# A mixer's attention steps spread over earlier products, and its branches taken attention by attention

## The chip, the cores and the metric

One core of a Trainium2 chip runs the whole program as a single launch. The metric is device time in microseconds (us). Of the kernel before, three runs were timed: 2173.23, 2173.37 and 2174.28, median 2173.37. One more execution was profiled; it took 2171.94.

## The reference, cut to what matters

The program is a stack of ten blocks on 256 tokens of width 1024: six of a first network (feed-forward, token mixer, feed-forward, twice) and four of a second one. The change touches only the token mixer, which runs twice (stages 1 and 4). A mixer has three attentions ("branches") on the same input, a gate for each, and one output projection:

```
proj = hn @ w_in                                   # q,k,v twice, c_q, c_kv, k_rope, gates
y_a = from_heads(moba_attention(partial_rope(qa), partial_rope(ka), va))      # 256 keys: a causal softmax
y_b = from_heads(stick_breaking_attention(qb, kb, vb))
qc = to_heads(rms_norm(c_q, q_norm) @ w_uq); kv = to_heads(rms_norm(c_kv, kv_norm) @ w_ukv)
y_c = from_heads(causal_softmax_attention(qc, [k_nope, kr], vc))
g = sigmoid(gates + b_gate)
merged = einsum('bsnk,nkd,bsnd->bsd', [y_a, y_b, y_c], w_branch, g)
return merged @ w_out
# stick breaking, per head, z = q k / 8, strictly earlier keys only:
log_1m = where(mask, log_sigmoid(-z), 0); suffix = reversed cumsum(log_1m) - log_1m
w = where(mask, exp(log_sigmoid(z) + suffix), 0);  y = w @ v
```

## The kernel before, in words

**Products.** Every weight arrives as 512 KB units of 128 x 1024 float32 (queue SP, line 81). ScalarE (ACT) rounds a unit to fp32r (`hi`, L122), VectorE (DVE) subtracts for the rest (`lo`, L127), and TensorE (PE) makes each product in three matmuls (L332 to L334). `lin2` does both halves of the 256 tokens against a block of four units: 8 chunks of the contraction, 6 matmuls each, so 12 matmuls a unit and 48 a block. `lin` does one half. Matmuls L332 to L334 are called "products" below; those of the latent projections are 384 or 416 columns wide, the others 512. Modulation vectors are made on DVE beside this (L422). Units are split ahead of their use as far as buffers allow.

**Queued steps.** What is not such a product is cut into steps (closures) in the queue `side`. `tick` runs the next step; `lin2` calls it once a unit, that is once in 12 products, unless its argument `fine` is set: then once in 6, and twice in 6 while the queue holds more than `backlog` steps. The order of instructions on every engine is fixed by the order in which this Python code issues them; engines run their own lists in order and wait on semaphores.

**A mixer** goes: q, k, v of attention 0 (three blocks), which queues its steps; q, k, v of attention 1, which queues the stick-breaking steps; the latent block (`lin2` with 416 columns), whose normed rows `cs` are transposed to `cT` (L374); gate block 0; the projections of the latent attention (`lin` with 384 and 512 columns in four rounds; queries `qs` and keys `ks` are transposed by L383 and copied by ACT); gate blocks 1 to 5; then twelve branch products (`branch(h, n, t)`: half `h` of the output columns, attention `n`, half `t` of the tokens); the transposes of the merged sum; and the output product.

**Softmax steps** (`softmax_steps`, attentions 0 and 2, three items each): score (PE L850, L853, maxima on DVE L876, eight or four exponentials on ACT L879), norm (DVE L887, L890), transposes of p (PE L383) with a copy (ACT L897), and the product with v (PE L913).

**Stick-breaking steps** (`stick_steps`, attention 1, two groups of four heads): three scores (PE L959, ACT L961, L962), one step for all three with Ln on ACT (L967), a sum on DVE (L968) and the mask product on GpSimd (POOL, L970); two empty steps (`yield`); then three steps with the triangular product (PE L976, L979, L980) and Exp (ACT L982); at the end two products with v (PE L991).

`branch` cannot start before its attention is ready; until then it runs queued steps back to back:

```
        def branch(h, n, t):
            while n not in ready:
                self.tick()
```

Of the kernel before, what the change touches and what calls it, by code (L numbers as in the profile page):

```python
# [15 lines left out]
AF = mybir.ActivationFunctionType  # L16
# [171 lines left out]
class Net:  # L188
# [759 lines left out]
    def stick_steps(self, groups, q_of, k_of, v_of, split):  # L948


        nc = self.nc
        w_of = {}
        for heads in groups:
            banks = [(1, heads, P, P), (0, heads[:2], 256, 0), (0, heads[2:], 256, 0)]
            zs, sps = [], []
            for kt, hs, w, q0 in banks:
                z = self.ps("acc")
                for i, h in enumerate(hs):
                    nc.tensor.matmul(z[:, i * w:(i + 1) * w], k_of(h, kt), q_of(h, q0, 256), start=i == 0, stop=False, skip_group_check=True)  # L959
                a = self.t2(name="sp")  # L960
                nc.scalar.activation(a, z, AF.Abs)  # L961
                nc.scalar.activation(a, a, AF.Exp, scale=-1.0)  # L962
                zs.append(z)
                sps.append(a)
                yield
            for (kt, hs, w, q0), z, a in zip(banks, zs, sps):
                nc.scalar.activation(a, a, AF.Ln, bias=1.0)  # L967
                nc.vector.scalar_tensor_tensor(out=a, in0=z, scalar=0.0, in1=a, op0=ALU.max, op1=ALU.add)  # L968
                d = a.rearrange("p (h q) -> p h q", q=w)[:, :, :P]
                nc.gpsimd.tensor_tensor(out=d, in0=d, in1=self.ustrict[:, None, :].broadcast_to([P, len(hs), P]), op=ALU.mult)  # L970
            yield
            yield
            for (kt, hs, w, q0), z, a in zip(banks, zs, sps):
                z3 = z.rearrange("p (h q) -> p h q", q=w)
                n = len(hs)
                nc.tensor.matmul(z, self.ntri, a, start=False, stop=False, skip_group_check=True)  # L976
                if kt == 0:
                    j = heads.index(hs[0])
                    nc.tensor.matmul(z3[:, :, P:], self.nones, sps[0].rearrange("p (h q) -> p h q", q=P)[:, j:j + n], start=False, stop=False, skip_group_check=True)  # L979
                nc.tensor.matmul(z3[:, :, :P], self.identb, self.m_causalT[:, None, :].broadcast_to([P, n, P]), start=False, stop=True, skip_group_check=True)  # L980
                e = self.t2(name="w")
                nc.scalar.activation(e, z, AF.Exp)  # L982
                for i, h in enumerate(hs):
                    w_of[h, kt] = e[:, i * w:(i + 1) * w]
                yield
        for m in range(2):
            yp = self.ps("acc")
            for c in range(2):
                for kt in range(NT):
                    for h in (4 * m + 2 * c, 4 * m + 2 * c + 1):  # L990
                        nc.tensor.matmul(yp[(h % 2) * 64:(h % 2) * 64 + 64, c * 256 + kt * P:(c + 1) * 256], v_of(h, kt), w_of[h, kt],  # L991
                                         start=kt == 0, stop=kt == 1, skip_group_check=True)
            self.soon(lambda m=m, yp=yp: split(m, yp), 1)
            yield

    def plan_mixer(self, st):
        l, A = st // 3, self.A
        blk = lambda b: [(A["w_mix"][l, b, u], U) for u in range(4)]
        w = []
        for b in range(6):  # L1000
            w += blk(b)
        w += [(A["w_mla"][l, u], 832) for u in range(4)] + blk(6)
        w += [(A["w_uq"][l, u], 768) for u in range(2)] + [(A["w_ukv"][l], U)]
        for b in range(7, 12):
            w += blk(b)
        for h in range(2):
            for n in range(3):
                w += [(A["w_branch"][l * 3 + n, h, u], U) for u in range(2)]
        return w + [(A["w_out"][l, k], U) for k in range(KC)]

    def mixer(self, st, pre, rest):
        nc = self.nc
        l = st // 3
        A = self.A
        self.reserve = 8
        hp = lambda h: slice((h % 2) * 64, (h % 2) * 64 + 64)
        par = lambda y: y.rearrange("p (c two d) -> p two c d", two=2, d=64)
        yTs, ready = {}, set()
# [16 lines left out]

        def put(n, i, ps, whole=False):

            if i == 0:
                yTs[n] = [self.s4([P, 4, 256], F32R, "yT") for _ in range(2)]
            if whole:  # L1040
                self.split_T(ps, *(a[:, 2 * i:2 * i + 2] for a in yTs[n]))
            else:
                self.split_T(ps, *yTs[n], i)
            if i:
                ready.add(n)

        def attend(n, q, k, v):

            if n == 0:
                self.both(self.softmax_steps(  # L1050
                    self.EVEN_ODD, lambda h, t: q[hp(h), h // 2, t * P:(t + 1) * P], lambda h, m: k[hp(h), h // 2, :m],
                    lambda: v, self.m_causal, lambda t, ps: put(n, t, ps)), lambda: self.free(q, k))
                self.side.append(lambda: self.free(v))
            else:
                gen = self.stick_steps(
                    [list(range(g, 8, 2)) for g in range(2)], lambda h, a, b: q[hp(h), h // 2, a:b],
                    lambda h, kt: k[hp(h), h // 2, kt * P:(kt + 1) * P], lambda h, kt: v[:, kt, h * 64:(h + 1) * 64], lambda m, ps: put(n, m, ps, True))
                self.steps(gen, 16)
                self.side.append(lambda: self.free(q, k))
                self.steps(gen, 2)  # L1060
                self.side.append(lambda: self.free(v))
# [5 lines left out]
        for n in range(2):  # L1067
            q, k = (self.s4([P, 4, 256], F32, "qkT") for _ in range(2))
            v = self.s4([P, NT, 512], F32, "v")
            if n == 0:  # L1070
                uq = self.get(4)
                end = rest(2)
                head(0, 0, self.lin(h8[0], uq), True, q)
                end()
                uk = self.get(4)
                head(1, 0, self.lin(h8[0], uk), True, k)
                self.trans(pre, 1)
                self.rate = 1
                head(0, 1, self.lin(h8[1], uq, drop=True), True, q)
                head(1, 1, self.lin(h8[1], uk, drop=True), True, k)  # L1080
            else:
                for i, dst in enumerate((q, k)):
                    for t, ps in enumerate(self.lin2(h8)):
                        head(i, t, ps, False, dst)
            for t, ps in enumerate(self.lin2(h8)):
                nc.scalar.copy(v[:, t], ps)
            attend(n, q, k, v)

# [3 lines left out]
        def gate(b):  # L1092
            h, n = divmod(b, 3)
            bg = self.t2(name="bg")
            nc.gpsimd.dma_start(bg, A["bgate"][l * 3 + n, h].partition_broadcast(P))
            g = self.s4([P, NT, 512], F32, "g")
            for t, ps in enumerate(self.lin2(h8)):
                nc.vector.tensor_tensor(out=g[:, t], in0=ps, in1=bg, op=ALU.add)
            gs[h, n] = g

# [4 lines left out]
        cs = [self.t2(name="cs") for _ in range(NT)]  # L1105
        css = self.sm(4, name="css")
        parts = [(0, 256), (256, 384)]
        for t, ps in enumerate(self.lin2(h8, 416)):
            nc.scalar.copy(cs[t][:, :416], ps[:, :416])
            junk = self.t2(name="junk")  # L1110
            for i, (a, b) in enumerate(parts):
                nc.scalar.activation(junk[:, a:b], cs[t][:, a:b], AF.Square, scale=(b - a) ** -0.5, accum_out=css[:, 2 * t + i:2 * t + i + 1])
# [22 lines left out]
        for hb in range(2):  # L1135
            for t in range(NT):
                c = lambda i: lambda k: [a[:, k + i, t * P:(t + 1) * P] for a in cT]
                ps = self.lin(c(0), wq, 384, 2, 1, hb * 384, 0)
                s = self.t2(name="qs")
                nc.scalar.activation(s[:, :384], ps[:, :384], AF.Copy, scale=96 ** -0.5)  # L1140
                sv = s[:, :384].rearrange("p (h d) -> p h d", h=4)[:, :, 64:96]
                self.rope(sv, sv, self.col("cosm", t * 32, 32), self.col("sinm", t * 32, 32), 4, 16)
                ps = self.lin(c(2), [wk], 512, 1, 1, hb * 512, 0)
                self.tick()
                pv = ps.rearrange("p (h d) -> p h d", h=4)
                z = self.t2(name="ks")
# [25 lines left out]
        def branch(h, n, t):  # L1172
            while n not in ready:
                self.tick()
            if (h, n) not in ub:
                ub[h, n] = self.get(2)
                nc.scalar.activation(gs[h, n], gs[h, n], AF.Tanh, scale=0.5)
            g = gs[h, n][:, t]
            ps = self.lin(lambda k: [a[:, k, t * P:(t + 1) * P] for a in yTs[n]], ub[h, n], 512, 4, 2)
            m = merged[t][:, h * 512:(h + 1) * 512]  # L1180
# [15 lines left out]
                self.split(pt.rearrange("p (k c) -> p k c", k=4), mT[0][q][s], mT[1][q][s], self.half)  # L1196
            self.free(merged[t])

        for n in range(3):
            for t in range(NT):  # L1200
                branch(0, n, t)
        for n in range(3):
            branch(1, n, 0)
        branch(1, 0, 1)
        mT = self.pair8("mT")
        mtrans(0)
        branch(1, 1, 1)
        branch(1, 2, 1)
        return self.proj_out(st, mT, lambda: mtrans(1))

# [965 lines left out]
```

## Time and profile before

| what | value |
|---|---|
| median of three runs | 2173.37 us |
| profiled execution, its own time | 2171.94 us |
| its span, first to last instruction | 2170.2 us |
| mean granted TensorE clock (1 is 2.4 GHz) | 0.975 |
| matmuls x9858, busy | 2050.8 us, 94% of the span |
| DVE busy | 1363.1 us, 63% |
| ACT busy | 917.4 us, 42% |
| DMA, mean rate | 274 GB/s |

The span is what the sums below move; 1.7 us lie around it. A busy share is a mean over stages. A timeline row gives the start, the duration, the engine, line, operation and tiles; in square brackets stands how long the engine had been idle before it and which instruction released it. Matmuls overlap, so a duration is a little longer than the distance to the next start.

### The profile page before, as it was taken

To read this page: it belongs to the slowest core of one execution; us is meant where nothing else is said; L and a number is where in the kernel's file an instruction comes from. 1 tells how busy PE (TensorE), PEld (TensorE's weight loads), DVE (VectorE), ACT (ScalarE), POOL (GpSimd) and SP (SyncE) were. 2 spreads that over 40 slices of the span, in tenths; PEclk is the share of its full clock that TensorE was granted. 3 is DMA by queue.
4 is the path that set the end of the run, shared out by engine and by line. 5 is a ranking of instruction groups with operands and counts; after the bars stand their busy time and mean duration, and the time that the engine had idled before them with its cause. 6 is when DMAs were issued, how large, how long until landed. Compare 5 with 4: busy or idle time off the path is not lost. (4 is left out here: it accounts for less than half of the span.)

```text
span 2170.2 us, 27088 instructions
## 1 busy us (share of the span) xinstructions
PE 2050.8 (94%) x9858; PEld 1437.9 (66%) x9858; DVE 1363.1 (63%) x2108; ACT 917.4 (42%) x1635; POOL 89.6 (4%) x118
## 2 busy tenths in 40 slices
PE   7999999988999999999989899998899989989998
PEld 4888777766888788777767688776533337763333
DVE  4976877558965886687647886697422258742223
ACT  3544454555544544355465544464211026621110
POOL 1000001000000000000000000030000002000000
PEclk9999999989999999999999999999899999989999
DMA  9987686527886787676635687666699996759998
GB/s 390 325 286 239 238 293 236 171 82 250 321 300 211 253 321 251 217 265 213 239 115 197 248 311 253 217 225 231 238 419 419 384 409 190 256 201 419 419 386 329
DMA packets 166956, 595.08 MB, mean 274 GB/s; under 512 B 18744, under 2 KB 18832, under 8 KB 166816
## 3 DMA queue, kind: packets, MB, share of 16 engines
q1 hardware_dynamic: 162864, 582.16, 72.8%
q0 software_dynamic: 2064, 6.88, 1.2%
q10 hardware_dynamic: 1888, 4.24, 0.6%
q8 instruction: 80, 1.31, 0.2%
q14 instruction: 60, 0.49, 0.1%
HBM read 590.00 MB, written 3.20 MB: 273 GB/s over the span
## 5 line engine op out<-in xcount | busy, mean ns | idle before, releaser
L127 DVE TENSOR_TENSOR lo<-raw,hi 128x1024 fp32r<-128x1024 f32 x478 | 570.3, 1214 | 37.0 <-ACT hi L122 35.5
L332 PE MATMUL psw<-hi,hT 128*128 128x512 f32 (+1 forms) x1296 | 525.8, 406 | 10.4 <-ACT hT L617 9.6
L334 PE MATMUL psw<-lo,hT 128*128 128x512 f32 (+1 forms) x1296 | 507.8, 392 | 5.9 <-DVE lo L127 5.8
L333 PE MATMUL psw<-hi,hT 128*128 128x512 f32 (+1 forms) x1296 | 507.6, 392 | 0.0
L122 ACT CAST hi<-raw 128x1024 fp32r<-128x1024 f32 x478 | 479.1, 1047 | 51.0 <-DMA raw<-in_w_gu_dram 16.9
L332 PEld LDWEIGHTS psw<-hi,hT 128*128 128x128 f32 x1296 | 244.7, 189 | 75.5 <-ACT hT L617 13.5
L334 PEld LDWEIGHTS psw<-lo,hT 128*128 128x128 f32 x1296 | 244.5, 189 | 59.6 <-DVE lo L127 8.5
L333 PEld LDWEIGHTS psw<-hi,hT 128*128 128x128 f32 x1296 | 245.2, 189 | 46.2
L422 DVE SCALAR_TENSOR_TENSOR aacc<-raw,csil,aacc 128x1024 f32<-128x1024 f32 x196 | 250.5, 1278 | 0.0
L1592 PE MATMUL psw<-raw,hg 128*64 128x512 f32 x1024 | 238.7, 605 | 5.7 <-PEq L2024 3.8
L1592 PEld LDWEIGHTS psw<-raw,hg 128*64 128x64 f32 x1024 | 69.0, 138 | 131.4 <-issue 122.5
L332 PE MATMUL psacc<-hi,gT 128*128 128x512 f32 x352 | 139.9, 397 | 6.0 <-ACT gT L725 3.1
L334 PE MATMUL psacc<-lo,gT 128*128 128x512 f32 x352 | 138.8, 394 | 1.0 <-DVE lo L127 1.0
L333 PE MATMUL psacc<-hi,gT 128*128 128x512 f32 x352 | 139.0, 395 | 0.0
L1636 DVE TENSOR_TENSOR x<-x,psacc 128x512 f32<-128x512 f32 x64 | 43.0, 686 | 121.3 <-PE psacc L1632 121.3
L1611 PE MATMUL psacc<-raw,gT 128*64 128x512 f32 x448 | 104.7, 598 | 0.4 <-DMA raw<-in_moe_d_dram 0.4
L688 ACT ACTIVATE sg<-psw 128x256 f32<-128x256 f32 x86 | 32.7, 384 | 153.9 <-PE psw L334 152.5
L557 POOL TENSOR_TENSOR r<-m,nhalf 128x1 f32<-128x1 f32 (+3 forms) x30 | 45.4, 1512 | 1218.1 <-DVE m L554 815.1
L689 DVE TENSOR_TENSOR sg<-psw,sg 128x256 f32<-128x256 f32 x86 | 35.9, 422 | 92.8 <-ACT sg L688 92.7
L725 ACT CAST gT<-psw 128x256 fp32r<-128x256 f32 x88 | 29.5, 375 | 130.0 <-PE psw L383 130.0
L332 PEld LDWEIGHTS psacc<-hi,gT 128*128 128x128 f32 x352 | 66.9, 190 | 22.1 <-ACT gT L725 4.8
L334 PEld LDWEIGHTS psacc<-lo,gT 128*128 128x128 f32 x352 | 66.9, 190 | 15.8 <-DVE lo L127 1.9
(331 smaller groups left out, 2314.1 us busy)
## 6 DMA issues: line engine op xcount, KB each, us to landing
raw<-in_ada_dram SPq DMA_DIRECT2D x224, 512.0 KB, 4.8
raw<-in_w_gu_dram SPq DMA_DIRECT2D x176, 512.0 KB, 4.9
raw<-in_moe_g_dram SPq DMA_DIRECT2D x128, 512.0 KB, 9.9
raw<-in_moe_u_dram SPq DMA_DIRECT2D x128, 512.0 KB, 9.9
raw<-in_moe_d_dram SPq DMA_DIRECT2D x128, 512.0 KB, 9.9
raw<-in_w_mix_dram SPq DMA_DIRECT2D x96, 512.0 KB, 4.6
raw<-in_w_dn_dram SPq DMA_DIRECT2D x88, 512.0 KB, 4.6
raw<-in_w_qkv_dram SPq DMA_DIRECT2D x48, 512.0 KB, 4.8
```

The lines of the kernel that those rows point to most:

```text
L122: nc.scalar.copy(hi[:, :cols], raw[:, :cols])
L127: nc.vector.tensor_tensor(out=lo[:, :cols], in0=raw[:, :cols], in1=hi.bitcast(F32)[:, :cols], op=ALU.subtract)
L332: mm(ps, a[0], w[0], start=first, stop=False)
L333: mm(ps, a[1], w[0], start=False, stop=False)
L334: mm(ps, a[0], w[1], start=False, stop=last)
L422: nc.vector.scalar_tensor_tensor(out=acc, in0=raw, scalar=c, in1=acc, op0=ALU.mult, op1=ALU.add)
L557: nc.gpsimd.tensor_tensor(out=r, in0=m, in1=self.nhalf[:, :w], op=ALU.pow)
L688: nc.scalar.activation(sg[:, :256], ps[:, :256], AF.Silu)
L689: nc.vector.tensor_tensor(out=sg[:, 256:], in0=ps[:, 256:], in1=sg[:, :256], op=ALU.mult)
L1592: mm(ps[s], hg(k, j)[:, s], w[0][:, i * 512:(i + 1) * 512], start=k == 0, stop=k == KC - 1)
L1611: mm(yb[h][s], gT[:, f * P + s.start:f * P + s.stop], w[0][:, h * 512:(h + 1) * 512], start=f == 0, stop=f == 3)
L1636: nc.vector.tensor_tensor(out=self.x[:, t, s], in0=self.x[:, t, s], in1=ps, op=ALU.add)
```

## The change

Six things, all in the mixer. The mixer's `lin2` calls get `fine=True`, with `backlog` 20, so a queued step runs after each 6 products, two while more than 20 wait. The first group of stick breaking has four empty steps in place of two between mask and triangular product. In the latent projections each `lin` runs a step at its middle and end. Branch products go attention by attention (both column halves of attention 0, then of 1, then of 2), with the weight units in that order, and both halves' gates go through tanh at once. The buffers of `yT` are taken by whichever part comes first.

```diff
-            yield
-            yield
+            for _ in range(4):
+                yield
...
-        for h in range(2):
-            for n in range(3):
+        for n in range(3):
+            for h in range(2):
                 w += [(A["w_branch"][l * 3 + n, h, u], U) for u in range(2)]
...
-        self.reserve = 8
+        self.reserve, self.backlog = 8, 20
...
-            if i == 0:
+            first = n not in yTs
+            if first:
                 yTs[n] = [self.s4([P, 4, 256], F32R, "yT") for _ in range(2)]
...
-            if i:
+            if not first:
                 ready.add(n)
...
-                self.steps(gen, 16)
+                self.steps(gen, 20)
...
-                    for t, ps in enumerate(self.lin2(h8)):
+                    for t, ps in enumerate(self.lin2(h8, fine=True)):
                         head(i, t, ps, False, dst)
...
-        for t, ps in enumerate(self.lin2(h8, 416)):
+        for t, ps in enumerate(self.lin2(h8, 416, fine=True)):
...
-                ps = self.lin(c(0), wq, 384, 2, 1, hb * 384, 0)
+                ps = self.lin(c(0), wq, 384, 2, 1, hb * 384, 1)
...
-                ps = self.lin(c(2), [wk], 512, 1, 1, hb * 512, 0)
+                ps = self.lin(c(2), [wk], 512, 1, 1, hb * 512, 1)
...
-                nc.scalar.activation(gs[h, n], gs[h, n], AF.Tanh, scale=0.5)
+                if h == 0:
+                    for i in range(2):
+                        nc.scalar.activation(gs[i, n], gs[i, n], AF.Tanh, scale=0.5)
...
-        for n in range(3):
-            for t in range(NT):
-                branch(0, n, t)
-        for n in range(3):
-            branch(1, n, 0)
-        branch(1, 0, 1)
+        for n in range(2):
+            for h in range(2):
+                for t in range(NT):
+                    branch(h, n, t)
+        branch(0, 2, 0)
+        branch(1, 2, 0)
         mT = self.pair8("mT")
+        branch(0, 2, 1)
         mtrans(0)
-        branch(1, 1, 1)
         branch(1, 2, 1)
```

Every engine has as many instructions as before. Three places show what moves; names carry the program's own tile numbers, and rows of the first mixer stand for both.

PE, second group of stick breaking, before: it stands behind the gate blocks, in the first branch products.

```order
L959 MATMUL psacc_3838<-qkT_2450,qkT_2451 128x128 x4
L959 MATMUL psacc_3846<-qkT_2450,qkT_2451 128x256 x2
L959 MATMUL psacc_3852<-qkT_2450,qkT_2451 128x256 x2
L976 MATMUL psacc_3838<-sp_3843,ntri 128x512
L980 LDWEIGHTS identb
L980 MATMUL psacc_3838<-m_causalT,identb 128x512
L976 MATMUL psacc_3846<-sp_3849,ntri 128x512
```

The same group in the changed kernel: its scores were issued 6 and 3 products apart, ahead of these rows, and this is the middle of the latent projections (`psw` from `cT`).

```order
L334 MATMUL psw_3259<-lo_3089,cT_2920 128x384
L383 MATMUL psw_3266<-ident,qs_3244 96x128 x4
L332 MATMUL psw_3279<-hi_3119,cT_2920 128x512
L333 MATMUL psw_3279<-hi_3119,cT_2921 128x512
L334 MATMUL psw_3279<-lo_3120,cT_2920 128x512
L383 MATMUL psw_3283<-ident,ks_3255 96x128 x4
L976 MATMUL psacc_3186<-sp_3191,ntri 128x512
L980 LDWEIGHTS identb
L980 MATMUL psacc_3186<-m_causalT,identb 128x512
```

Before, nothing stands between last score and first triangular product; now 15 products do, 12 of them ahead of the transposes of `qs_3244`.

ACT, latent projections, before: only copies and scalings of the projections.

```order
L1140 ACTIVATE qs_3115<-psw_3108 128x384
L442 COPY zs_3131<-psw_3126 128x256
L1148 COPY ks_3133<-psw_3122 128x4x64
L1140 ACTIVATE qs_3144<-psw_3137 128x384
L1148 COPY ks_3164<-psw_3151 128x4x64
```

ACT, the same place in the changed kernel, with the stick steps of the second group ahead of the first scaling (L1141 was L1140).

```order
L961 ACTIVATE sp_3229<-psacc_3226 128x512
L962 ACTIVATE sp_3229<-sp_3229 128x512
L967 ACT_TABLE_LOAD
L967 ACTIVATE sp_3191<-sp_3191 128x512
L967 ACTIVATE sp_3212<-sp_3212 128x512
L967 ACTIVATE sp_3229<-sp_3229 128x512
L1141 ACTIVATE qs_3244<-psw_3222 128x384
L1149 COPY ks_3255<-psw_3251 128x4x64
```

The scaling that the transposes of `qs_3244` need now follows the Ln passes of the third score.

ACT, first softmax item of attention 0, before: v's two copies are out of the way before its exponentials.

```order
L1086 COPY v_2098<-psw_2350 128x512
L1086 COPY v_2098<-psw_2351 128x512
L122 CAST hi_2464<-raw_2413 128x1024
L442 COPY zs_2481<-psw_2476 128x256
L122 CAST hi_2492<-raw_2440 128x1024
L879 ACT_TABLE_LOAD
L879 ACTIVATE p_2519,rs_2504<-psacc_2505,mx_2517 128x128 x4
```

ACT there in the changed kernel (L1087 was L1086): the score was issued 6 products before v's block ends.

```order
L1087 COPY v_2098<-psw_2350 128x512
L1087 COPY v_2098<-psw_2351 128x512
L879 ACT_TABLE_LOAD
L879 ACTIVATE p_2487,rs_2472<-psacc_2473,mx_2485 128x128 x4
L879 ACTIVATE p_2494,rs_2472<-psacc_2474,mx_2492 128x128 x4
```

The exponentials now wait for the end of v's block; on PE the transposes of this item follow its score after 18 products and one further score, where it was 48 products.

## Rows read from the trace of the kernel before

**Rows 1.** Windows of the second mixer: us, busy PE, PEld, DVE, ACT, POOL, clock, DMA, GB/s.

```profile
932.00:1096.00 164.00, 161.83 (x840) 129.33 (x839) 117.07 (x158) 86.16 (x150) 7.04 (x12) 1.00 0.70 241
1096.00:1166.00 70.00, 59.52 (x309) 44.45 (x308) 37.74 (x53) 41.98 (x80) 5.28 (x6) 0.90 0.26 91
```

**Rows 2.** PE's waits in a mixer, by releaser: us in total, times, longest.

```profile
PE psacc L976 <- POOL sp L970: 6.6, 2, 5.9
PE psw L332 <- DVE cT L374: 2.7, 1, 2.7
```

**Rows 3.** Timeline of PE, second mixer, from the second stick group to the branches.

```profile
1106.16 2.88 PE L959 MATMUL psacc<-qkT,qkT 64*128 64x128 f32 x16
1114.97 2.08 PE L976 MATMUL psacc<-sp,ntri 128*128 128x512 f32 x2 [5.92 <-POOL sp L970]
...
1121.33 2.82 PE L991 MATMUL psacc<-w,v 128*64 128x256 f32 x32
1124.08 0.50 PE L332 MATMUL psw<-hi,yT 128*128 128x512 f32 x1
...
1126.96 1.95 PE L850 MATMUL psacc<-qkm,qkm 96*128 96x128 f32 x16
...
1131.91 1.89 PE L850 MATMUL psacc<-qkm,qkm 96*128 96x256 f32 x8
...
1133.90 1.23 PE L383 MATMUL psw<-ident,p 128*128 128x128 f32 x8
...
1148.01 0.80 PE L332 MATMUL psw<-hi,yT 128*128 128x512 f32 x1
...
1150.31 0.41 PE L334 MATMUL psw<-lo,yT 128*128 128x512 f32 x1
```

**Rows 4.** Timeline of PE, second mixer: the same kinds of step at full pace.

```profile
982.76 1.13 PE L850 MATMUL psacc<-qkT,qkT 64*128 64x256 f32 x8
983.82 0.39 PE L853 MATMUL psacc<-m_causal,identb 128*128 128x256 bf16 x2
986.82 1.03 PE L383 MATMUL psw<-ident,p 128*128 128x128 f32 x8
...
1008.80 1.09 PE L913 MATMUL psacc<-pT,v 128*64 128x128 f32 x16
1009.82 0.50 PE L332 MATMUL psw<-hi,hT 128*128 128x512 f32 x1
...
1104.67 1.02 PE L976 MATMUL psacc<-sp,ntri 128*128 128x512 f32 x2
```

**Rows 5.** Timeline of ACT and POOL behind those scores, up to the masks.

```profile
1110.92 1.28 ACT L967 ACT_TABLE_LOAD   x1
1112.22 1.67 ACT L967 ACTIVATE sp<-sp 128x512 f32<-128x512 f32 x3
...
1113.65 2.63 POOL L970 TENSOR_TENSOR sp<-sp,ustrict 128x512 f32<-128x512 f32 x3 [13.01 <-DVE sp L968]
```

**Rows 6.** Groups of instructions in the second mixer: count, busy us, mean ns, idle before.

```profile
L879 ACT ACTIVATE p<-psacc,mx 128x128 f32<-128x128 f32 x16 | 5.6, 376 | 4.7 <-DVE mx L876 4.7
L968 DVE SCALAR_TENSOR_TENSOR sp<-psacc,sp 128x512 f32<-128x512 f32 x6 | 3.8, 684 | 12.8 <-ACT sp L967 12.8
L1086 ACT COPY v<-psw 128x512 f32<-128x512 f32 x4 | 2.3, 594 | 0.6 <-PE psw L334 0.5
```

**Rows 7.** Timeline of PE, first mixer: the product behind the wait for `cT`.

```profile
340.25 0.44 PE L332 MATMUL psw<-hi,cT 128*128 128x384 f32 x1 [2.72 <-DVE cT L374]
```

**Rows 8.** A window of the first mixer after that wait; columns as in rows 1.

```profile
341.00:345.00 4.00, 4.00 (x19) 2.35 (x18) 2.93 (x12) 1.14 (x3) 1.01 (x4) 0.57 0.30 120
```

**Rows 9.** Timelines of POOL and DVE: one small POOL operation at two places, and DVE beside it.

```profile
1008.21 2.01 POOL L557 TENSOR_TENSOR r<-m,nhalf 128x4 f32<-128x4 f32 x1 [69.86 <-DVE m L554]
...
1008.03 1.29 DVE L422 SCALAR_TENSOR_TENSOR aacc<-raw,csil,aacc 128x1024 f32<-128x1024 f32 x1
...
1513.57 1.01 POOL L557 TENSOR_TENSOR r<-m,nhalf 128x4 f32<-128x4 f32 x1 [25.38 <-DVE m L554]
```

More of the change, by code (lines that the diff above doesn't have):

```diff
@@ L1082, in mixer @@
                 for i, dst in enumerate((q, k)):
-                    for t, ps in enumerate(self.lin2(h8)):
+                    for t, ps in enumerate(self.lin2(h8, fine=True)):
                         head(i, t, ps, False, dst)
-            for t, ps in enumerate(self.lin2(h8)):
+            for t, ps in enumerate(self.lin2(h8, fine=True)):
                 nc.scalar.copy(v[:, t], ps)
@@ L1096, in gate @@
             g = self.s4([P, NT, 512], F32, "g")
-            for t, ps in enumerate(self.lin2(h8)):
+            for t, ps in enumerate(self.lin2(h8, fine=True)):
                 nc.vector.tensor_tensor(out=g[:, t], in0=ps, in1=bg, op=ALU.add)
```

## The prediction

> **What bounds the kernel.** I read the page's busy shares first: TensorE (PE) 94%, DVE 63%, ACT 42%. PE sets the time, so a microsecond is to be had only where PE waits or runs at a low clock. The windows of a mixer say where that is. In its front, 164 us of weight products, PE is busy 161.8 us at clock 1.00; in the 70 us behind it, where the queue is emptied and the branches run, PE is busy 59.5 us at clock 0.90 [rows 1]. PE's waits by releaser name two kinds in a mixer that the change touches: 6.6 us for the masks of stick breaking (two waits, one of them 5.9) and 2.7 us for `cT` [rows 2]. The timeline shows the rest: in the second mixer the last stick group starts at 1106.16 and its final products end as branch products begin at 1124.08; the latent softmax runs from 1126.96 to 1148.01; the five products behind it start 0.43 to 0.6 us apart, where twelve in a row at full pace take 2.88 (1124.08 to 1126.96), 0.24 each [rows 3]. Those stretches are what the change can win: each holds steps that wait for a chain through ACT, DVE and POOL with nothing else left for PE. The first mixer shows the same waits, so I count everything twice.
>
> **What the change gives.** It puts these steps among earlier products, where they should cost their pace alone. Per mixer:
> - Stick group 2: 17.92 us elapsed (1106.16 to 1124.08) [rows 3]. At pace: scores 2.88, three products with their masks at 1.49 each (1104.67 to 1106.16) [rows 3, 4], final products 2.82: 10.2 together. Gain 7.7; 5.92 of it is the wait, the rest half-pace work behind it.
> - Latent softmax: 21.05 elapsed, less 2.88 for twelve products inside it, 18.17. At pace: three scores at 1.99 each (1131.91 to 1133.90), three transposes at 1.03, three products with v at 1.09 [rows 3, 4]: 12.3. Gain 5.8.
> - The five slow products: 2.30 (1148.01 to 1150.31) against 1.20: gain 1.1.
> - Group 1's wait: 6.6 - 5.9 = 0.7, counted whole here; what stays of it stands below.
> - Each return to the product stream costs a longer first product, 0.50 where others have 0.41 [rows 3, 4]. Steps that stood back to back now return one by one, some 16 more breaks: 16 x 0.1 = 1.6 lost.
>
> Sum 7.7 + 5.8 + 1.1 + 0.7 - 1.6 = 13.7; two mixers 27.4.
>
> **What it costs.** A step costs only its pace if enough products stand between its halves. At twice the rate there are half as many between two steps. I go through the places by the issue order and compare the cover with the chain.
> - *First softmax item, attention 0.* The chain: six products to the end of v's block 1.4, two copies of v 2 x 0.59, a table load 1.28, eight exponentials at 0.376, two DVE passes at 0.68 [rows 5, 6]: 1.4 + 1.2 + 1.3 + 3.0 + 1.4 = 8.3. The cover in the first mixer: 18 products (4.3) and a further score, 1.13 + 0.39 [rows 4], 5.8. PE waits 2.5. A wait of such a size is not its own whole price: behind the 2.72 us for `cT` in the first mixer [rows 7] the granted clock stands at 0.57 for four microseconds [rows 8], near the 1.2 GHz level, which loses 4 x 0.43 = 1.7. So 2.5 + 1.7 = 4.2. In the second mixer 24 products (5.8 + 1.5 = 7.3) leave 1.0. Together 5.2.
> - *Stick group 1.* Four empty steps at one per 6 products equal two at one per 12: 24 products both times. The 0.7 stays, and the products are now those of 416 columns; I add 0.8. 1.5 x 2 = 3.0.
> - *The wait for `cT`.* It lies at the same block's end and its chain is the same; what stands between now differs by a step or two. Zero, between -4.4 (2.72 + 1.7 won) and +4.4.
> - *Stick group 2, in the latent projections.* Its bare chain (ACT, the table, three Ln, DVE's sum, POOL's masks) cost 5.92 of waiting where nothing covered it. In the first mixer only 12 narrow products stand ahead of transposes which need a scaling that ACT does behind the Ln passes: about 0.19 each by width, 2.3. It leaves 3.6, with the clock 1.7: 5.3. In the second mixer 18 narrow products and sums cover about 4.6: 1.3. Together 6.6.
> - *Latent softmax.* It now competes with DVE's splits and modulation sums. Such a sum takes 1.28 and may start ahead of a normalization: between 0 and 1.28 each time, taken 0.9 per mixer. 1.8.
> - *tanh of both halves at once* delays a copy on ACT by one half's length; the branch products hold several finished PSUM tiles ahead. Nothing; if a tile is missing, one tanh per attention.
> - *The weight units' order* changes which 512 KB unit comes when, not how many; in the tail DMA is 0.26 busy [rows 1]. Nothing.
>
> Sum 5.2 + 3.0 + 0 + 6.6 + 1.8 = 16.6.
>
> *Does DVE become the bound?* Its steps move from the tail to the front: two groups' sums, maxima, normalizations, copies, some 15 us per mixer (22 passes of 0.68). 117.1 us of 164 [rows 1] become 132 of about 185, 72% (the front is longer by the PE steps it takes in). Not on average.
>
> One pair of rows speaks against putting masks beside splits: a POOL operation, 128x4, shows 2.01 us where a DVE pass of 1.29 lies beside it and 1.01 where it has POOL and DVE to itself [rows 9]. So a POOL operation can lose about one DVE pass. The Trainium skill ("SBUF — State Buffer", section "SBUF: two separate sides") says that VectorE and GpSimd share a port pair under an exclusive lock, held for the whole instruction by whichever began first; the two durations agree with it. By the row, four groups have three masks each, so 12 x 1.28 = 15.4 us at worst. I leave it out of the sum: the first mask of a group stands behind a DVE sum that must end first anyhow, and the chains above are not late by one pass at every mask. It is a rival below.
>
> **Sum.** 27.4 - 16.6 = 10.8 us won: 2171.94 - 10.8 = 2161.1 for the profiled execution. The median of the runs is 1.4 above it, so **2162.5, say 2162**. What is uncertain in this case: the wait for `cT` (4.4 either way) and the clock's 1.7 at two waits, 3.4: its own range is 2154 to 2170.
>
> **Rivals** (all against the median).
> - *Everything is covered.* The chains were measured with queues full of other work; if they fit, the 16.6 vanish: 2173.4 - 27.4 = 2146, and with the `cT` wait gone as well 2141.6. For it: front PE is never without work, and splits stand two to five units ahead. Against: the cover of 2.3 us at stick group 2 is far under 5.92.
> - *DVE serves the queue late.* Engines go in order; a DVE sum that waits for ACT's table and Ln (1.28 + 1.67 [rows 5]) holds the splits behind it, and PE waits for a `lo`. Four groups, up to 2.95 each, 11.8; half of it, 5.9, gives 2168, all 2174. For: the splits' lead is short in places. Against: a unit of 12 products lasts 2.9, so a lead of two hides one such delay.
> - *Slower.* One mechanism: bare chains now stand in the front six times where they stood in the tail twice. The four stick groups and two first softmaxes each cost the bare 5.92 and the 1.7 of low clock, 7.6 x 6 = 45.6, plus 1.8 for the latent softmax, against 27.4: 20 us lost, 2193. It decides from (27.4 - 1.8) / 6 = 4.3 us for each of the six. Against: at five of the six 18 or more products stand between, 3.4 us or more of 5.9 to 8.3. I take its middle, 5.5 each (33 + 1.8 against 27.4): 2181.
> - *POOL and DVE slow each other.* The 15.4 us at the masks takes the 10.8 and a little more: 2173 if two thirds reach PE, 2178 if all do. Against: the masks cover part of each other's wait.
> - *It does not do what it says.* The queue may be emptied in the front, so that the same waits stand in front of the gates rather than after: no gain, 2171 to 2175. The order shows steps between products at both places, which speaks against it.
>
> **Chances.** Forecast case 0.48, all covered 0.16, DVE late 0.11, slower 0.12, POOL beside DVE 0.05, no effect 0.08. The measurement can tell about 0.2%, 4.3 us, so "same" is 2169.1 to 2177.7. Faster takes the forecast case but 0.03 of its upper edge, the covered case, and 0.09 of the late DVE: 0.45 + 0.16 + 0.09 = 0.70. Slower: the mechanism 0.12 and 0.01 of POOL beside DVE, 0.13. Same: the rest, 0.17. The range: low 2143, inside the covered case (0.06 of it left out), high 2175, which leaves out the slower cases' 0.13: 0.81 inside.
>
> **What would show it.** In the profile after, the tail's window (branches and output) should be near 1.00 of clock with no wait at L976, L383 or L913; the L976 wait for POOL should stand in the latent projections at 3 to 4 us in the first mixer, and a wait for p (L383 behind DVE L890) of 2 to 3 us near the first softmax. With everything covered, neither would be there. DVE late shows as PE waiting at L334 for `lo`; POOL beside DVE as masks well over the 0.88 us that each of three takes now (2.63 for three [rows 5]) and longer waits at L976. The slower case has six waits of over 4 us and a clock under 0.95 in the front. A mean front clock under 0.97, or a tail that still lasts 70 us, would make my account wrong whatever the time.

## The result, and the profile after

The changed kernel takes 2148.11 us (median of six, 2146.56 to 2154.43) against 2174.89 for the kernel before on the same chips (six, 2173.23 to 2177.83): ratio 0.9883, interval 0.9873 to 0.9894, about 25 us faster. The forecast was 2162, some 11 us faster, in a range of 2143 to 2175. The side and the range hold; the gain is more than twice what was forecast. The profiled execution took 2150.40, 21.5 less than that of before.

The page after, its busy times: the instructions and their cost are as before, the span is shorter.

```profile
span 2148.7 us, 27125 instructions
PE 2046.8 (95%) x9858; PEld 1436.9 (67%) x9858; DVE 1364.8 (64%) x2108; ACT 918.9 (43%) x1635; POOL 93.4 (4%) x118
```

The second mixer by windows, with the columns of [rows 1]: from 72 us behind its start, as there, to its branches, then the branches. These begin 28 us later in the mixer than before.

```profile
925.00:1116.00 191.00, 187.81 (x1019) 147.13 (x1018) 134.02 (x185) 118.40 (x219) 14.16 (x18) 1.00 0.63 211
1116.00:1150.00 34.00, 33.91 (x155) 27.94 (x154) 29.48 (x36) 17.80 (x19) 0.00 (x0) 1.00 0.60 218
```

The tail that PE spent at clock 0.90 with 10 us idle is now 34 us without a gap at 1.00; the stretch ahead of it is longer by the steps it took in, and DVE is busy 70% there (134.02 of 191), as estimated.

PE's waits in the mixers after, by releaser (us, times, longest), first mixer, then second; rows of the mixers' start, equal in both kernels, are left out.

```profile
PE psw L383 <- DVE qs L839: 4.9, 1, 4.9
PE psw L332 <- ACT zs L442: 2.0, 1, 2.0
...
PE psacc L976 <- POOL sp L970: 0.7, 1, 0.7
```

```profile
PE psw L440 <- ACT qs L1141: 1.4, 1, 1.4
...
PE psacc L976 <- POOL sp L970: 0.7, 1, 0.7
PE psw L383 <- DVE p L890: 0.6, 1, 0.6
...
PE psw L332 <- DVE g L1099: 0.5, 1, 0.5
```

Against [rows 2], the 5.9 at L976 and the wait for `cT` are gone in both mixers, and so are two kinds of wait in the tail that [rows 2] does not list, 2.4 at L913 and 1.5 at L383 for `p`; a new one of 4.9 stands at the transposes of `qs`, in the first mixer alone.

Where the time went is best read from PE's timeline, between the same rows in every kernel: *front*, from the last L483 ahead of the mixer to the first product on `cT`; *latent*, to the last on `cT`; *gates*, to the first on `yT`; *branches*, to the last on `yT`; *next*, from the last on `mT` to the next stage's L483. The output product between takes 22.6 or 22.7 everywhere. Each pair is first mixer / second.

| kernel | front | latent | gates | branches | next | sum with output |
|---|---|---|---|---|---|---|
| before | 111.7 / 159.9 | 10.9 / 9.0 | 67.2 / 67.0 | 74.6 / 75.9 | 68.0 / 69.8 | 355.1 / 404.2 |
| changed | 124.0 / 174.8 | 20.8 / 15.8 | 78.6 / 73.1 | 33.6 / 33.6 | 68.4 / 68.5 | 348.1 / 388.6 |
| old branches | 124.9 / 174.7 | 21.4 / 17.5 | 78.6 / 73.1 | 33.3 / 33.3 | 70.5 / 70.3 | 351.4 / 391.6 |
| coarse | 111.7 / 159.9 | 16.8 / 15.0 | 73.8 / 68.8 | 56.7 / 56.7 | 67.6 / 68.4 | 349.2 / 391.5 |
| two empty | 127.7 / 175.9 | 23.5 / 21.8 | 73.1 / 74.5 | 33.6 / 33.6 | 67.8 / 67.7 | 348.4 / 396.2 |
| quiet latent | 123.8 / 174.7 | 10.3 / 9.5 | 79.8 / 82.0 | 33.7 / 33.6 | 68.0 / 68.4 | 338.2 / 390.9 |
| late ticks | 123.7 / 174.7 | 19.8 / 16.2 | 78.5 / 73.1 | 33.6 / 33.7 | 68.5 / 67.3 | 346.8 / 387.6 |
| quiet, no double | 122.9 / 172.9 | 9.8 / 9.8 | 87.6 / 86.9 | 33.7 / 33.6 | 67.6 / 68.4 | 344.3 / 394.3 |
| order only | 111.4 / 160.0 | 10.8 / 9.0 | 67.2 / 66.9 | 73.0 / 72.9 | 68.4 / 68.4 | 353.5 / 399.9 |
| quiet first | 123.7 / 174.7 | 10.3 / 15.8 | 79.8 / 73.1 | 33.6 / 33.6 | 68.0 / 68.4 | 338.1 / 388.4 |

The two mixers with their next stages give 22.6 us (7.0 and 15.6); the branches alone lose 41.0 and 42.3, of which 33.6 and 27.9 come back as longer front, latent and gates. A second trace of the changed kernel, taken with the last experiments, has the same parts within 0.2, but for *next* in the second mixer (67.3).

### The profile page after: what moved, and what is told of

It is laid out like the page before. It is cut to its first block, busy times and chain, and to the rows that moved or that the text cites. A ratio compares the mean times of both kernels' runs of the same rounds, so it can differ in the third digit from the quotient of the medians.

```text
span 2148.7 us, 27125 instructions
## 1 busy us (share of the span) xinstructions
PE 2046.8 (95%) x9858; PEld 1436.9 (67%) x9858; DVE 1364.8 (64%) x2108; ACT 918.9 (43%) x1635; POOL 93.4 (4%) x118
## 5 line engine op out<-in xcount | busy, mean ns | idle before, releaser
L122 ACT CAST hi<-raw 128x1024 fp32r<-128x1024 f32 x478 | 480.8, 1048 | 91.6 <-PE psw L333 23.5
L1596 PEld LDWEIGHTS psw<-raw,hg 128*64 128x64 f32 x1024 | 68.6, 137 | 131.1 <-issue 122.9
L332 PEld LDWEIGHTS psacc<-hi,gT 128*128 128x128 f32 x352 | 67.4, 192 | 20.1 <-ACT gT L725 6.2
L333 PEld LDWEIGHTS psacc<-hi,gT 128*128 128x128 f32 x352 | 67.5, 192 | 16.1 <-DVE gT L727 2.4
```

Of the source, the lines that this page charges most:

```text
L122: nc.scalar.copy(hi[:, :cols], raw[:, :cols])
L332: mm(ps, a[0], w[0], start=first, stop=False)
L333: mm(ps, a[1], w[0], start=False, stop=False)
L1596: mm(ps[s], hg(k, j)[:, s], w[0][:, i * 512:(i + 1) * 512], start=k == 0, stop=k == KC - 1)
```

## Experiments

**Branches in the old order** (e1): branches, weight units and tanh as before, all else changed.

```diff
...
-        for n in range(2):
-            for h in range(2):
-                for t in range(NT):
-                    branch(h, n, t)
...
+        for n in range(3):
+            for t in range(NT):
+                branch(0, n, t)
+        for n in range(3):
+            branch(1, n, 0)
...
```

> The changed kernel with the old order of branches, of their weight units and of the tanh. Theory (the fine steps alone empty the queue before the gates end, so no branch waits for anything): 2148, between 2146 and 2151; no wait at L976, L913 or at L383 for p among the branch products. Rival (attention by attention is what gives the cover): 2158 or more, with waits of 2 us and more back between the gates and the output product.

Measured 2156.12, ratio 0.9912 (0.9899 to 0.9926): outside both. The theory's reason holds, since the branches have no wait and are even 0.3 shorter (33.3), but its number does not. Of the 6.3 that its mixers lose in the table, 3.9 stand in the *next* stage, 2.1 and 1.8. PE's waits there, from 515 to 535 us, of this kernel and then of the changed one:

```profile
PE psw L334 <- DVE lo L127: 3.0, 2, 2.2
PE psacc L332 <- ACT hi L122: 1.4, 1, 1.4
```

```profile
PE psw L383 <- DVE sg L689: 2.6, 1, 2.6
PE psacc L332 <- ACT gT L725: 0.5, 1, 0.5
```

With the old order the next stage's products wait for `lo` and `hi`. These waits go with the order and not with the length of the tail, for the kernel before has them too (518 to 538 us):

```profile
PE psw L334 <- DVE lo L127: 3.5, 2, 2.1
PE psacc L332 <- ACT hi L122: 1.5, 1, 1.5
```

There the clock is 1.00 through the whole *next* part, and it takes 68.0; in the old-order kernel the clock is 0.93 and it takes 70.5. Another 1.7 is in the second mixer's latent part, where the same short waits as in the changed kernel are followed by slow products here and not there (last section).

**Paired branches** (e6): the old order, but both token halves of attention 0 in a row for the second column half, and the first transposes of the merged sum one branch later. Against the kernel above:

```diff
-        for n in range(3):
-            branch(1, n, 0)
-        branch(1, 0, 1)
+        for t in range(NT):
+            branch(1, 0, t)
         mT = self.pair8("mT")
-        mtrans(0)
+        branch(1, 1, 0)
+        branch(1, 2, 0)
         branch(1, 1, 1)
+        mtrans(0)
         branch(1, 2, 1)
```

> The kernel with the old order of branches (2156), but for the second column half both token halves of attention 0 are taken in a row, so two units are given back before the next four come; the rest of the old order, weight order and tanh, stays. Theory (the old order is slower because it holds six branch units at once, so that transfers stop for 6 us in the branches and the next stage's first splits come late): transfers stop for less, 2150 to 2153, with the next stage's first PE waits between those of the two. Rival (the tanh order or the grouping by attention costs it on ACT or DVE): 2155 to 2158.

Measured 2155.88, ratio 0.9916 (0.9903 to 0.9930), with the very waits of e1 in the next stage. At most four units are held at once here, and nothing is won; the theory falls. Whether it is the tanh, the order of the units or where the gates' and `yT`'s buffers come free stays open.

**Order only** (e8): the kernel before with the new order of branches, units and tanh; nothing else changed.

```diff
...
-        for h in range(2):
-            for n in range(3):
+        for n in range(3):
+            for h in range(2):
                 w += [(A["w_branch"][l * 3 + n, h, u], U) for u in range(2)]
...
+        for n in range(2):
+            for h in range(2):
+                for t in range(NT):
+                    branch(h, n, t)
...
```

> The kernel before with the new order of branches, weight units and tanh alone; steps once per 12 products, two empty steps, nothing in the latent projections. Theory (the order gives little cover while the queue is full: 6 products more ahead of group 2's masks, and the long branches leave transfers time anyway): 2173.5 less 2 to 4, that is 2169 to 2172, with a wait of 4 to 5 us at L976 in each mixer. Rival (the order is worth by itself what undoing it cost, 6 to 8): 2165 to 2168.

Measured 2166.47, ratio 0.9966 (0.9952 to 0.9979). The rival is right about the amount: alone the order gives about 7, and taken away from the change it costs about 6. With the 19 that the changed kernel keeps in the old order (e1), the two nearly add up to the 25 of the whole. The places differ. Here the branches are shorter by 1.6 and 3.0: the longest wait at L976 in the first mixer is 3.8 where it was 5.9, as products of attention 0's second half stand between.

**Coarse pace** (e2): one step per 12 products.

```diff
...
-                    for t, ps in enumerate(self.lin2(h8, fine=True)):
+                    for t, ps in enumerate(self.lin2(h8)):
...
-        for t, ps in enumerate(self.lin2(h8, 416, fine=True)):
+        for t, ps in enumerate(self.lin2(h8, 416)):
```

> The changed kernel with one queued step per 12 products in the mixers again; four empty steps, the steps in the latent projections and the branch order stay. Theory (the pace is worth only what it keeps off the tail, and costs what it puts into the latent projections): the second stick group is covered by some 60 products of the gates and first branches, so its 7.7 stays won and the wait of 4.9 for the scaling of qs with its low clock (together about 6.6) and mixer 2's 2.1 go; the end of the latent softmax is bare again, about 6 per mixer: 2148 + 12 - 9 = 2151, between 2147 and 2155. Rival (the fine pace carries the whole gain): 2165 to 2174.

Measured 2156.33, ratio 0.9913 (0.9900 to 0.9927): just above the theory's range, far from the rival. The fine pace is worth 6 to 8 us of the 25 (by the ratios and by the medians). The wait for `cT` is back in the first mixer, between 330 and 345 us:

```profile
PE psw L332 <- DVE cT L374: 2.7, 1, 2.7
```

This is the term I had put at zero: at the fine pace the transposes of `cs` come while products of gate block 0 are still to be issued, at the coarse one right ahead of the projections that need them. PE in the changed kernel, then here:

```profile
345.47 0.49 PE L383 MATMUL psw<-ident,cs 128*128 128x128 f32 x3
...
352.52 0.45 PE L332 MATMUL psw<-hi,cT 128*128 128x384 f32 x1
```

```profile
338.51 0.81 PE L383 MATMUL psw<-ident,cs 128*128 128x128 f32 x6
342.05 0.45 PE L332 MATMUL psw<-hi,cT 128*128 128x384 f32 x1 [2.73 <-DVE cT L374]
```

One wait for a `lo` in the gates (3.4) had not been expected.

**Two empty steps** (e3).

```diff
-            for _ in range(4):
+            for _ in range(2):
                 yield
...
-                self.steps(gen, 20)
+                self.steps(gen, 16)
```

> The changed kernel with two empty steps between masks and triangular product, as before. Theory: group 1 loses 6 products of cover per mixer, 1.4 more of waiting at L976 each; in group 2 the wait moves from the transposes of qs to L976, 5 to 6 us in the first mixer and about 4 in the second where it was 2: together 2148 + 3 + 1 + 2 = 2154, between 2150 and 2158. Rival (the empty steps are idle weight at this pace): 2148, within 2.

Measured 2159.88, ratio 0.9930 (0.9916 to 0.9943). The theory's waits are there, in sum a little smaller than expected; L976 in the first mixer, then in the second (the second group's are 4.1 and 2.8):

```profile
PE psacc L976 <- POOL sp L970: 6.8, 2, 4.1
```

```profile
PE psacc L976 <- POOL sp L970: 4.6, 2, 2.8
...
PE psw L332 <- ACT pT L897: 2.5, 2, 2.2
```

Together 11.4 at L976 where the changed kernel has 1.4 there and 6.3 for `qs`. The time is 2 above the range; the low clock behind the longer waits (0.57 over the four microseconds behind the 2.8) and the 2.2 at `pT` in the second mixer had not been counted. The two more empty steps are worth some 10 us, more than the fine pace.

**Quiet latent projections** (e4): no step inside them; one a round stays.

```diff
-                ps = self.lin(c(0), wq, 384, 2, 1, hb * 384, 1)
+                ps = self.lin(c(0), wq, 384, 2, 1, hb * 384, 0)
...
-                ps = self.lin(c(2), [wk], 512, 1, 1, hb * 512, 1)
+                ps = self.lin(c(2), [wk], 512, 1, 1, hb * 512, 0)
```

> The changed kernel without the steps at the middle and end of each latent projection; one step a round stays, behind the scaling of qs. Theory (the one large stall left is the scaling of qs on ACT behind the table load and Ln, and the rotation of qs on DVE behind the sums): the wait of 4.9 with its low clock, about 6.6, goes in the first mixer and 2.1 in the second; the second group's masks then have over 30 products of cover: 2148 - 8.5 = 2139.5, between 2137 and 2143, no wait over 1 us in the latent projections. Rival (the chain is simply too long for any place near the projections, and the wait turns up at L976 or at the latent softmax): 2146 to 2150.

Measured 2141.93, ratio 0.9849 (0.9835 to 0.9862), inside the theory's range. In the first mixer the latent part falls from 20.8 to 10.3, and the whole by 9.9. One wait over 1 us stays in each mixer's latent projections, 1.5 and 1.4, where the theory had none. Of the second mixer it was wrong: that is 2.3 longer. Its latent part gives 6.3, but its gates are 8.9 longer, and two transposes of `p` wait there for tiles that DVE's gate additions free, which stand behind a normalization and its maxima:

```profile
PE psw L383 <- DVE g L1099: 1.5, 2, 1.0
```

ACT, DVE, POOL and PE in the latent projections, changed kernel: what the transposes at 361.74 waited for.

```profile
355.75 1.28 ACT L967 ACT_TABLE_LOAD   x1
357.05 1.67 ACT L967 ACTIVATE sp<-sp 128x512 f32<-128x512 f32 x3
358.62 0.47 ACT L1141 ACTIVATE qs<-psw 128x384 f32<-128x384 f32 x1
```

```profile
357.71 1.89 DVE L968 SCALAR_TENSOR_TENSOR sp<-psacc,sp 128x512 f32<-128x512 f32 x3 [4.29 <-ACT sp L967]
359.51 0.45 DVE L836 TENSOR_TENSOR rp<-qs,cv 128x128 f32<-128x128 f32 x1
359.89 0.81 DVE L837 TENSOR_TENSOR rp<-qs,cv 128x128 f32<-128x128 f32 x1
360.73 0.63 DVE L838 TENSOR_TENSOR qs<-rp 128x64 f32<-128x64 f32 x1
361.28 0.31 DVE L839 TENSOR_TENSOR qs<-rp 128x64 f32<-128x64 f32 x1
```

```profile
358.56 2.72 POOL L970 TENSOR_TENSOR sp<-sp,ustrict 128x512 f32<-128x512 f32 x3 [16.53 <-DVE sp L968]
```

```profile
361.74 1.06 PE L383 MATMUL psw<-ident,qs 128*96 128x128 f32 x4 [4.88 <-DVE qs L839]
```

Table load and Ln first, then the scaling; on DVE the sums, then the rotation of `qs`. The same rotation in the quiet kernel, ahead of the sums and with POOL idle:

```profile
355.63 0.29 DVE L836 TENSOR_TENSOR rp<-qs,cv 128x128 f32<-128x128 f32 x1 [1.04 <-ACT qs L1141]
355.84 0.28 DVE L837 TENSOR_TENSOR rp<-qs,cv 128x128 f32<-128x128 f32 x1
356.16 0.22 DVE L838 TENSOR_TENSOR qs<-rp 128x64 f32<-128x64 f32 x1
356.31 0.22 DVE L839 TENSOR_TENSOR qs<-rp 128x64 f32<-128x64 f32 x1
```

**Late ticks** (e5): four steps a round, but behind the scaling and behind the copies.

```diff
-                ps = self.lin(c(0), wq, 384, 2, 1, hb * 384, 1)
+                ps = self.lin(c(0), wq, 384, 2, 1, hb * 384, 0)
...
-                ps = self.lin(c(2), [wk], 512, 1, 1, hb * 512, 1)
-                self.tick()
+                self.tick(2)
+                ps = self.lin(c(2), [wk], 512, 1, 1, hb * 512, 0)
...
                 nc.gpsimd.tensor_copy(zv[:, :, 64:], kr[t][:, None, :].broadcast_to([P, 4, 32]))
+                self.tick(2)
```

> The changed kernel with as many steps in the latent projections, four a round, but two of them issued behind the scaling and rotation of qs and two behind the copies of ks, instead of inside the projections. Theory (at four steps a round the chain of table load, Ln, sums and masks has some 9 to 18 narrow products, 2 to 3 us, where it needs about 6, whatever stands ahead of it on ACT): the wait moves from the transposes of qs to those of ks or to L976 and stays at 3 us or more in the first mixer: 2143 to 2149. Rival (only the place of the scaling behind Ln on ACT counts): no wait over 1 us, 2138 to 2142 as with the quiet projections.

Measured 2150.26, ratio 0.9890 (0.9875 to 0.9905): no different from the changed kernel, and 1.3 above the theory's range. The wait has moved to the transposes of `ks`, as the theory said; their copies on POOL stand behind the masks. PE and POOL there:

```profile
356.47 0.60 PE L383 MATMUL psw<-ident,qs 128*96 128x128 f32 x4
361.83 1.09 PE L383 MATMUL psw<-ident,ks 128*96 128x128 f32 x4 [4.06 <-POOL ks L1151]
```

```profile
358.81 2.67 POOL L970 TENSOR_TENSOR sp<-sp,ustrict 128x512 f32<-128x512 f32 x3 [16.99 <-DVE sp L968]
361.43 0.84 POOL L1151 COPY ks<-kr 128x128 f32<-128x128 f32 x3
```

So the place on ACT is not what counts: with four steps a round the wait only finds another engine. That the quiet version mends it by the number of products between agrees with this.

**Quiet, never two steps at once** (e7): e4 with the limit for double steps out of reach.

```diff
-        self.reserve, self.backlog = 8, 20
+        self.reserve, self.backlog = 8, 10 ** 6
```

> The kernel with quiet latent projections (2142), and never two steps at once. Theory (steps now end 18 to 24 products ahead of the branches even so, and group 1's masks get 30 to 36 products instead of 24): the two waits of 0.7 at L976 go with what is behind them: 2140, between 2137 and 2142. Rival (the queue needs the double steps): steps left for the branches, 2146 or more.

Measured 2151.39, ratio 0.9895 (0.9880 to 0.9910): the rival's time, but not by its reason, for the branches stay at 33.7 and 33.6 without a wait. The front gains 0.9 and 1.8, but the gates lose 7.8 and 4.9. In the first mixer PE waits there for splits:

```profile
PE psw L334 <- DVE lo L127: 3.6, 2, 2.0
```

In the second it waits 4.0 for DVE's gate additions. This is the prediction's rival "DVE serves the queue late", in a kernel other than the one it was written for. How it comes from single steps was not traced further.

**Beside one another** (e9, e10, e11): the changed kernel, the quiet one, and one with no step at all in the latent projections, which against the quiet one is

```diff
-                self.tick()
                 pv = ps.rearrange("p (h d) -> p h d", h=4)
```

> The changed kernel itself, beside the two that follow and the kernel before on one chip, so that they can be compared directly: ratio 0.988 to before, as it was (0.9873 to 0.9894); if it is nearer to 0.985, the quiet projections gained nothing.

> The kernel with quiet latent projections (one step a round) once more, beside the changed kernel: 6 to 10 us less than it. If the gain seen first was the chip's, within 2 us.

> No step at all in the latent projections. Theory (in the quiet version the Ln step of the round still stands ahead of the next scaling of qs, and a product waits 1.5 for it in each mixer; without a step that wait goes, and the gates have room for four more steps): 2 to 4 us less than the quiet version. Rival (the steps pushed into the gates make DVE late, as where never two steps ran at once): 2 us or more above the quiet version, with waits for lo in the gates.

Measured 2148.82, 2143.22 and 2145.58; ratios 0.9886 (0.9869 to 0.9902), 0.9854 (0.9837 to 0.9871) and 0.9862 (0.9846 to 0.9879). The quiet version's gain over the changed kernel repeats, 5.6 by the medians, a little under what was expected; the two intervals just touch here, and lay apart the first time. The silent one cannot be told from the quiet one: its first mixer has a wait of 3.2 for `lo` in the gates, which its rival named, and its second mixer does without the two waits at L383.

**Quiet in the first mixer alone** (e12). `l` is 0 in the first mixer and 1 in the second.

```diff
-                ps = self.lin(c(0), wq, 384, 2, 1, hb * 384, 1)
+                ps = self.lin(c(0), wq, 384, 2, 1, hb * 384, l)
...
-                ps = self.lin(c(2), [wk], 512, 1, 1, hb * 512, 1)
+                ps = self.lin(c(2), [wk], 512, 1, 1, hb * 512, l)
```

> The changed kernel with quiet latent projections in the first mixer alone; the second keeps its steps there. Theory (the traces of both show the quiet version 9.7 to 9.9 us shorter in the first mixer, and 2.3 to 2.8 longer in the second, where only 2 us of waiting stood to be won and later normalizations came late): 2 to 3 us less than the quiet version, ratio to before 0.9835 to 0.9845; first mixer 338 and second 387 to 389 by its trace. Rival (what the second mixer loses comes from the first mixer's order, through the transfers): second mixer 390 or more, ratio 0.985 or more.

Measured 2139.95 (2139.46 to 2141.48), ratio 0.9842 (0.9829 to 0.9856), with 338.1 and 388.4 by its trace, as the theory has it. It beats the kernel before and, the intervals being apart, the changed one. Over the quiet version it gains 1.9 and 2.6 in the traces; the ratios' intervals overlap.

## Why the prediction was right, and too small

The mechanism was right: the tail's waits and low clock go, the same steps cost little among products, and the largest new wait stands where the sum put it, at the second stick group in the first mixer's latent projections. Of the signs, the tail's clock came true; the wait said to show at L976 with 3 to 4 us came at the transposes of `qs` with 4.88, and the one of 2 to 3 us near the first softmax did not come.

The size was wrong. The forecast's own range, 2154 to 2170, was missed; the time lies 2 above "everything is covered" (2146) and 14 under the forecast, and is in the stated range because that reached into this rival. The sum was 27.4 - 16.6 = 10.8; the trace has 22.6. Term by term, for two mixers:

- *The wait for `cT`*, taken as zero between -4.4 and +4.4: gone in both mixers. In the first that is 2.72 and 1.7 of low clock; in the second 0.8, and a wait of 1.2 for a scaled `qs` in its front, which had no term, went too. **6.4 won**, the largest miss. The step that failed is "what stands between now differs by a step or two"; e2 brings the wait back by the pace alone.
- *First softmax item*, 5.2: measured 0 in the first mixer and 0.6 in the second. The chain was put together wrongly. I read the score as issued 6 products before v's block ends; it stands 6 products into the next block, and v's copies (272.17 to 273.44) are over before the score begins (274.34). ACT after, around them:

```profile
272.17 1.27 ACT L1087 COPY v<-psw 128x512 f32<-128x512 f32 x2 [0.92 <-PE psw L334]
273.46 1.28 ACT L879 ACT_TABLE_LOAD   x1
276.59 0.37 ACT L879 ACTIVATE p<-psacc,mx 128x128 f32<-128x128 f32 x1 [1.85 <-DVE mx L876]
```

  The table load, too, lay in time in which ACT had to wait for the maxima. The transposes began at 281.41 without a wait, behind a normalization that ended at 281.05: it fits by 0.4 us. **4.6 better.**
- *Stick group 1*, 3.0: the waits of 0.66 and 0.67 stay; the 0.8 each for narrower products did not come. **1.7 better.**
- *Stick group 2*, 6.6: 4.88 and, at clock 0.80 from its end to 370.00, 1.7 in the first mixer; 1.42 and 0.46 in the second. 8.5, **1.9 worse**. The bare chain of 5.92 was the right row; I missed that the rotation runs at half speed beside POOL.
- *Latent softmax*, 1.8: nothing at its own transposes in the first mixer, but a product waits 1.95 for a PSUM tile whose copy (`zs`, L442) stands on ACT behind eight exponentials and a `hi`, which is not the reason forecast, and the clock falls behind it. 3.5 there, none in the second: **1.7 worse**. Windows of the wait and of the four microseconds after it:

```profile
392.00:396.00 4.00, 2.05 (x14) 1.27 (x7) 4.00 (x5) 4.00 (x16) 0.00 (x0) 0.96 0.85 291
396.00:400.00 4.00, 4.00 (x13) 3.11 (x12) 1.86 (x5) 0.95 (x2) 0.15 (x1) 0.61 0.37 123
```

10.8 + 6.4 + 4.6 + 1.7 - 1.9 - 1.7 = 19.9, 2.7 short of the trace. Of these, 0.9 is won in the next stages, which had no term. The rest falls, by difference, to the first sum: the branches lose 83.3 in both mixers, front, latent and gates gain 61.5, and the terms above make 7.5 of that; so the steps themselves took 54.0, and moving them won 29.3 where 27.4 stood. What breaks in the product stream cost (3.2 had been charged) is inside the 54.0, and no run measures it by itself.

*The order of branches, weight units and tanh* had no term of its own: units and tanh were costed at nothing, the units with the tail's idle DMA as cover. e1 shows the three together worth 6 us with the change in place, and e8 shows 7 without it; which of the three it is stays open. A long tail is no cover for the next stage's splits, since the kernel before has the waits for `lo` and `hi` there.

*Rivals.* "Everything is covered" is nearest, yet not all is: three waits of 1.4 to 4.9 stand. POOL beside DVE exists as a mechanism, but it was DVE that was slowed, for 1.2 us. The slower case and a late DVE did not come; the latter does in e7, and in single waits in e2 and e11.

## What to carry to other kernels

Where a queue of steps is emptied in a place without other work, spreading it wins most of the wait, and each step then needs as many microseconds of independent work behind it as its chain lasts: count products by width, since twelve narrow ones are 2 us. Read the order of instructions together with their times before adding up a chain: copies and table loads that are done before the chain begins are no part of it. A change of order that is costed at nothing deserves a run of its own: here it was worth 6 to 7 us, with the spreading and without.

## What had not been expected of the hardware

DVE's rotation passes, 128x128 with two SBUF inputs, take 0.28 to 0.29 us with POOL idle and 0.45 and 0.81 beside POOL's masks; the two of half width take 0.22 and then 0.63 and, beside POOL's copies of `ks`, 0.31. The four sum to 1.0 and to 2.2, on the path that ended PE's longest wait. Where a later round meets the masks in the quiet kernel and in the one with late ticks, the full-width passes take 0.83 and 0.81 each. The masks themselves, 2.72 for three, are hardly slower than in [rows 5] (2.63). The Trainium skill ("SBUF — State Buffer", section "SBUF: two separate sides") has, for a VectorE operation with two SBUF inputs and a GpSimd one that reads SBUF, the engine that comes second blocked for the whole of the other's instruction; a DVE pass held back by up to one mask agrees with it. The prediction had drawn the wrong side from it: masks waiting for splits, where here the short DVE passes waited for masks.

The same short waits were followed by a lower clock in some kernels and not in others. In the second mixer's latent projections, waits of 1.42 and 0.46 leave the granted clock at 1.00 over the six microseconds behind them in three traces with the new order (the changed kernel twice, quiet first). Both traces with the old order (e1 and e6) have the same two waits there, and a clock of 0.72 behind them, with products half again as long. Windows of the changed kernel, then of e1:

```profile
1032.00:1038.00 6.00, 5.97 (x31) 4.52 (x32) 3.48 (x12) 3.98 (x8) 2.28 (x6) 1.00 0.02 4
```

```profile
1037.00:1043.00 6.00, 5.74 (x23) 4.10 (x24) 2.58 (x9) 3.45 (x7) 1.82 (x4) 0.72 0.02 5
```

So 1.7 us of what the old order costs is clock, in a place that lies ahead of the mixer's own branches. What decides between the two is not shown.
